# Sixteen experts on 64 slots and two column strips, sixteen on 32 slots and four, with the overflow branch moved behind the sixth quad

## Chip, cores and metric

One NeuronCore of a Trainium2 chip runs the whole program. The metric is device microseconds of one execution, as the median of the runs shown.

## The reference, cut to what matters

Two layers of mixers and a dense feed-forward run first, and then two more layers, each of which ends in a mixture of 32 experts. Only that expert stage is touched. For 256 tokens of width 1024 a router picks one of four groups and in it the two best of eight experts:

```python
def expert_block(args):
    xblk, e = args
    hid = jax.nn.silu(xblk @ w_gate[e]) * (xblk @ w_up[e])
    return hid @ w_down[e]

contrib = weights[order][:, None] * yb[dest]
y = jnp.zeros((t, d)).at[sorted_tok].add(contrib)
```

Gate and up are 1024x512, down is 512x1024, all in float32: 6 MB for one expert, 192 MB for a layer. The 512 assignments of a layer (256 tokens by 2) fall on the 32 experts as the data has it.

## The kernel before

**Slots.** The kernel gives each expert 32 slots (CAP, line 61). Four experts (a quad) share the 128 columns of TensorE: the gathered tokens of expert j are the stationary operand of column strip j (32 columns), and its weights stream through as the moving operand, 512 columns at a time. Each such product is two instructions in the trace. Line 1587 holds gate (`g`) and up (`u`), line 1615 down (`yp`).

**A quad** (`moe`, from line 1520) runs so: `prep` builds a 0/1 matrix `sel` of tokens by slots on VectorE (line 1528) and gathers the tokens with it on TensorE (line 1542, tile `xt` in PSUM, two buffers of tag x); VectorE and ScalarE move the result into `XT` in turn, with the layer's scale and shift (lines 1546, 1548). There is one XT, so the next quad's can be filled only when the last `u` product has read it. `up` makes gate and up, with `combine` of the quad before between them (tile `cb`, line 1635, eight products, added into x by VectorE). `turn` transposes sel (tile `cT`). `hidden` transposes the hidden layer (tile `hTp`, line 1601, also in a buffer of tag x), `down` multiplies it, and `halves` scales the result and splits it in two.

**The weights' stream.** A ring of 1 MB tiles (class Ring, line 181) is filled by SyncE in the order that `plan_second` (line 1115) lists: for each quad gate, up and down, each in two halves of four tiles, one by expert: 24 tiles a quad, 192 a layer. A tile's transfer (line 214) is issued when the tile that many places back has been released, which `done` does behind each half: four tiles at a time. In the expert stage the ring's pools are RING, RING1, RING2 and RING3 (3, 6, 4 and 4 tiles). The first quad has extra work of the layer norm behind its `up` (`late`, line 1876: four products `rowb`, ScalarE copies, GpSimd scaling).

**The branch.** An expert with more than 32 tokens spills. `weights` in `route` (line 1498) leaves the two largest counts and their experts in `mi`. Behind the third quad (XAT = 3, line 49) every engine reads them, and if the largest is over 32, `overflow` (line 1678) loads the weights of those two experts a second time (24 transfers of 0.5 MB, tile `fw`, line 1711) and treats up to 64 further tokens of each on two column strips, through the same `up`, `down` and `combine`. `rest` (line 1723) is for what then still remains. The first gather behind the branch can't be done ahead. In the order of SyncE's queue the branch stands between two of the ring's transfers.

Of the kernel before, what the change touches and what calls it, by code (L numbers as in the profile page):

```python
# [11 lines left out]
F32 = mybir.dt.float32  # L12
F32R = mybir.dt.float32r
# [3 lines left out]
ALU = mybir.AluOpType  # L17
# [3 lines left out]
P = 128  # L21
S = 256
D = 1024
KT = D // P
NT = S // P
# [14 lines left out]
NP = 2  # L40
RING1 = 6
RING2 = 4
RING3 = 4
DP = ((0, 100), (2000, 0))
WB = (0, 0, 3)
PB = (2, 3, 3)
EV = 'avaa'
RINGX = (0, 1)
HIPB = 4
XAT = 3  # L50
HQ = 2
HT = 0
LAG = 2
# [4 lines left out]
HF = 4  # L58
NE = 32
DE = 512  # L60
CAP = 32
QE = 4
XCAP = 64
KEY = 64
ALPHA = (2.0 * DEPTH) ** 0.25
# [10 lines left out]
class Packer:  # L76
# [3 lines left out]
    def add(self, name, width):  # L80
        self.at[name] = (self.n, width)
        self.n += width


def const_layout():
# [162 lines left out]
def v3(a, b):  # L248
    return lambda t: t[:, : a * b].rearrange("p (a b) -> p a b", a=a)


class Kern:
# [60 lines left out]
    p = c  # L313
# [801 lines left out]
    def plan_second(self, i):  # L1115
        ap, ring = self.ap, self.ring
        if i == 0:
            ring.rows(ap["norm_final"])
            w = ap["a_w_in_2"][0].rearrange("(k p) c -> p k c", p=P)
            for g in range(4):  # L1120
                for h in range(2):
                    ring.add((w[:, :, h * D + g * 256 : h * D + (g + 1) * 256], v3(8, 256)))
            wo = ap["a_w_out_2"][0]
        else:
            w = ap["b_w_in_2"][0].rearrange("(k p) c -> p k c", p=P)
            for g in range(4):
                for h in (1, 2, 0):
                    ring.add((w[:, :, h * D + g * 256 : h * D + (g + 1) * 256], v3(8, 256)))
            wo = ap["b_w_out_2"][0]
        wo = wo.rearrange("(k p) c -> p k c", p=P)  # L1130
        for kk in range(4):
            ring.add((wo[:, 2 * kk : 2 * kk + 2, :], v3(2, D)))
        ring.blank()
        for qd in range(NE // QE):
            if qd == NE // QE - 1:
                ring.blank()
            es = range(QE * qd, QE * qd + QE)
            for nm in ("e_w_gate_2", "e_w_up_2"):
                for hf in range(2):
                    for e in es:  # L1140
                        ring.add((ap[nm][i, e].rearrange("(p k) f -> p k f", p=P)[:, 4 * hf : 4 * hf + 4, :], v3(4, DE)))
            for hf in range(2):
                for e in es:
                    ring.add((ap["e_w_down_2"][i, e].rearrange("(p f) d -> p f d", p=P)[:, 2 * hf : 2 * hf + 2, :], v3(2, D)))

    def affine(self, pool, g, b, sc, sh):
        nc = self.nc
# [291 lines left out]
    def route(self, i, pool, pC, rw, csum, crow, stats, meanwhile):  # L1439
        nc = self.nc  # L1440
# [10 lines left out]
        key = pool.tile([P, NE], F32, name="key")  # L1451
# [66 lines left out]
        return R, W, (key, k8, mi), weights  # L1518

    def moe(self, i, pool, A, B, R, W, g1, xs, weights, late, pG, pU, pY, pX, pC):  # L1520
        nc = self.nc
# [10 lines left out]
            return last  # L1532

        def gather(sel):
            XT = v3(KT, P)(pool.tile([P, KT * P], F32, name="XT", tag="XT"))
            for q in range(KT // 4):
                b = pX.tile([P, 4, P], F32, name="xt", tag="x")
                for k in range(4):
                    c0 = (4 * q + k) * P
# [3 lines left out]
                for k in range(4):  # L1543
                    kk = 4 * q + k
# [6 lines left out]
        def slots():  # L1551
            return pool.tile([P, NT, P], F32R, name="sel", tag="sel", bufs=2)

        def prep(qd, then=None):
            sel = slots()
            last = pick(sel, QE, CAP, R, slice(QE * qd, QE * qd + QE))
# [91 lines left out]
            if end and i < DEPTH - 1:  # L1648
                self.scale_x(rows)

        def take(tag, at):
            return (2 if tag == "d" else 4), [self.ring.take() for _ in range(QE)]

        cur = prep(0, weights)
        pend = None
        for qd in range(NE // QE):
# [10 lines left out]
            if qd == 0:  # L1667
                with self.after(last):
                    late()
                src = self.row_src(self.ap["ffn_ln_g_2"][i], self.ap["ffn_ln_b_2"][i])  # L1670
            C, ws = turn(sel, QE, CAP, lambda t, j: W[:, t, QE * qd + j : QE * qd + j + 1])
            if qd + 1 < NE // QE and qd + 1 != XAT:
                cur = prep(qd + 1)
            pend = (C, halves(down(hidden(sl), QE, CAP, take, self.ring.done), ws))
        combine(*pend, end=True)
        self.ring.drop(held)

    def overflow(self, i, pool, A, B, R, W, g1, xs, pG, pU, pY, pX, pC, fns):
        nc, tc = self.nc, self.tc
        pick, gather, slots, turn, up, hidden, down, halves, combine = fns  # L1680
        key, k8, mi = xs
        over = (CAP + 1) * KEY
        rv = nc.values_load(mi[0:1, 2:3], min_val=0, max_val=(S + 1) * KEY)
        with tc.If(rv > over):
            es = [nc.values_load(mi[0:1, j : j + 1], min_val=0, max_val=NE - 1) for j in range(2)]
            oh = pool.tile([P, 2, NE], F32, name="oh", tag="oh")
# [2 lines left out]
            for j in range(2):  # L1689
                nc.vector.tensor_scalar(oh[:, j, :], key, k8[:, j : j + 1], None, op0=ALU.is_equal)  # L1690
                for t in range(NT):
                    nc.vector.scalar_tensor_tensor(junk, R[:, t, :], 1.0, oh[:, j, :], ALU.mult, ALU.mult, accum_out=Rx[:, t, j : j + 1])
                    nc.vector.scalar_tensor_tensor(junk, W[:, t, :], 1.0, oh[:, j, :], ALU.mult, ALU.mult, accum_out=Wy[:, t, j : j + 1])
            nc.vector.tensor_scalar(Rx, Rx, float(-CAP), None, op0=ALU.add)
            sel = slots()
# [23 lines left out]
            gv = nc.values_load(mi[0:1, 3:4], min_val=0, max_val=(S + 1) * KEY)  # L1719
            with tc.If(gv > over):  # L1720
                self.rest(i, pool, A, B, R, W, g1, key, oh, pG, pU, pY, pX)

    def rest(self, i, pool, A, B, R, W, g1, key, oh, pG, pU, pY, pX):
        nc, tc = self.nc, self.tc
        if True:
            scr = pool.tile([P, 7 * NE], F32, name="scr", tag="yl")
# [6 lines left out]
            nc.vector.tensor_scalar(thr, thr, float(XCAP), float(CAP + 1), op0=ALU.mult, op1=ALU.add)  # L1733
# [14 lines left out]
            for t in range(NT):  # L1748
# [3 lines left out]
                    nc.tensor.transpose(b, self.n[:, t, k::KT], self.ident)  # L1752
                    nc.vector.tensor_scalar(h[:, k, :], b, A[:, k : k + 1], B[:, k : k + 1], op0=ALU.mult, op1=ALU.add)
                with tc.For_i(0, NE, 1) as iv:
                    ce = nc.values_load(mi[0:1, 0:1], min_val=-KEY * XCAP, max_val=(S + 1) * KEY)
                    with tc.If(ce > (CAP + 1) * KEY):
# [246 lines left out]
```

## Time and profile before

| | us |
|---|---|
| median of 3 runs (2137.33 to 2144.72) | 2140.43 |
| the profiled execution, its own time | 2138.41 |
| its span in the profile | 2136.6 |
| TensorE busy, share of the span | 1817.5, 85% |
| VectorE busy | 943.2, 44% |
| ScalarE busy | 578.9, 27% |
| read from memory over the span | 607.24 MB, 285 GB/s |

Engines in the rows: PE is TensorE, DVE is VectorE, ACT is ScalarE, POOL is GpSimd, SPq is the queue of SyncE. A row's L number is a line of the kernel. "PEclk" is TensorE's granted clock as a share of 2.4 GHz. The span is the profiler's window of the execution; its times are counted from the span's start.

### The profile page before, as it was taken

How to read it: one execution, taken by the hardware profiler on the slowest of the kernel's cores; microseconds unless marked ns; L12 is line 12 of the kernel's file. 1: busy time of each engine (PE TensorE's matmuls, PEld its weight loads, DVE VectorE, ACT ScalarE, POOL GpSimd, SP SyncE). 2: the span in 40 equal slices, each digit the busy share in tenths (PEclk: the TensorE clock that was granted, in tenths of full speed). 3: DMA queues.
4: the chain of work that ended last, by engine and by line, in shares of the span. 5: the costliest groups of instructions: out<-in, count | busy, mean ns of one | idle time of the engine just before them, and what ended most of it. 6: DMA issues, size and time to landing. Idle time of an engine off the chain costs nothing. (4 is left out here: it accounts for less than half of the span.)

```text
span 2136.6 us, 27574 instructions
## 1 busy us (share of the span) xinstructions
PE 1817.5 (85%) x10962; PEld 1210.9 (57%) x10962; DVE 943.2 (44%) x1935; ACT 578.9 (27%) x1120; POOL 179.0 (8%) x219
## 2 busy tenths in 40 slices
PE   7999999999989997898875588777799977777875
PEld 7887999998879996765312133222398421422221
DVE  6565779564677786874111011111486310111112
ACT  5443544263454332333100010001234200100010
POOL 2210000020100004400100000000240100000000
PEclk9787999996889997997987799999799799799888
DMA  7222979351368993565999659999947699999996
GB/s 221 76 99 80 339 276 375 107 153 37 108 225 284 327 340 122 160 222 215 422 422 423 220 199 423 423 423 422 364 171 302 265 423 422 390 423 422 423 422 271
DMA packets 181708, 611.09 MB, mean 286 GB/s; under 512 B 19392, under 2 KB 105792, under 8 KB 132416
## 3 DMA queue, kind: packets, MB, share of 16 engines
q1 hardware_dynamic: 178368, 605.05, 73.8%
q10 hardware_dynamic: 1872, 2.26, 0.3%
q0 software_dynamic: 1328, 1.90, 0.3%
q8 instruction: 89, 1.46, 0.3%
q14 instruction: 51, 0.42, 0.1%
HBM read 607.24 MB, written 1.93 MB: 285 GB/s over the span
## 5 line engine op out<-in xcount | busy, mean ns | idle before, releaser
L372 DVE TENSOR_TENSOR wlo<-w,whi 128x1024 fp32r<-128x1024 f32 (+3 forms) x232 | 277.5, 1208 | 101.0 <-ACT whi L371 100.1
L371 ACT CAST whi<-w 128x1024 fp32r<-128x1024 f32 (+3 forms) x232 | 224.3, 983 | 230.3 <-PE gu L406 59.4
L1587 PE MATMUL u<-w,XT 128*32 128x512 f32 x1024 | 201.1, 697 | 75.8 <-DMA w<-in_e_w_up_dram 75.7
L1595 DVE TENSOR_TENSOR sl<-sl,u 128x512 f32<-128x512 f32 x17 | 11.7, 687 | 504.7 <-PE u L1587 504.7
L1587 PE MATMUL g<-w,XT 128*32 128x512 f32 x1024 | 191.0, 658 | 33.6 <-DMA w<-in_e_w_gate_dram 33.6
L1615 PE MATMUL yp<-w,sl 128*32 128x512 f32 x1024 | 198.1, 657 | 18.3 <-DMA w<-in_e_w_down_dram 12.8
L1587 PEld LDWEIGHTS u<-w,XT 128*32 128x32 f32 x1024 | 44.5, 125 | 220.4 <-DMA w<-in_e_w_up_dram 139.6
L407 PE MATMUL gu<-hTf,wlo 128*128 128x256 f32 x512 | 146.5, 286 | 0.7 <-DVE wlo L372 0.6
L405 PE MATMUL gu<-hTf,whi 128*128 128x256 f32 x512 | 146.2, 286 | 0.8 <-ACT whi L371 0.8
L406 PE MATMUL gu<-hTf,whi 128*128 128x256 f32 x512 | 145.8, 285 | 0.0
L1625 DVE SCALAR_TENSOR_TENSOR y<-yp,ws,g 128x512 f32<-128x512 f32 x34 | 25.5, 749 | 252.8 <-PE yp L1615 235.4
L1615 PEld LDWEIGHTS yp<-w,sl 128*32 128x32 f32 x1024 | 48.8, 117 | 139.1 <-issue 88.8
L1587 PEld LDWEIGHTS g<-w,XT 128*32 128x32 f32 x1024 | 44.0, 118 | 135.3 <-issue 67.4
L807 DVE SCALAR_TENSOR_TENSOR aacc<-w,ca,aacc 128x1024 f32<-128x1024 f32 x84 | 107.5, 1280 | 2.2 <-DMA w<-in_ada_w_dram 1.5
L405 PEld LDWEIGHTS gu<-hTf,whi 128*128 128x128 f32 x512 | 98.3, 192 | 2.7 <-ACT whi L371 1.2
L406 PEld LDWEIGHTS gu<-hTf,whi 128*128 128x128 f32 x512 | 98.9, 193 | 1.4
L407 PEld LDWEIGHTS gu<-hTf,wlo 128*128 128x128 f32 x512 | 98.1, 192 | 2.4 <-DVE wlo L372 1.1
L1542 PE MATMUL xt<-sel,nhh 128*128 128x128 f32 x272 | 86.1, 340 | 13.3 <-DVE sel L1528 13.3
L1548 ACT ACTIVATE XT<-xt,B,A 128x128 f32<-128x128 f32 x68 | 28.9, 455 | 242.0 <-DVE XT L1546 240.7
L405 PE MATMUL mm<-whi,hT 128*128 128x384 f32 (+2 forms) x256 | 88.8, 354 | 4.6 <-ACT hT L489 4.6
L1542 PEld LDWEIGHTS xt<-sel,nhh 128*128 128x128 f32 x272 | 67.8, 249 | 38.5 <-issue 32.5
L406 PE MATMUL mm<-wlo,hT 128*128 128x384 f32 (+2 forms) x256 | 89.3, 352 | 0.0
(488 smaller groups left out, 3687.7 us busy)
## 6 DMA issues: line engine op xcount, KB each, us to landing
w<-in_e_w_gate_dram SPq DMA_DIRECT2D x128, 1024.0 KB, 19.7
w<-in_e_w_up_dram SPq DMA_DIRECT2D x128, 1024.0 KB, 19.7
w<-in_e_w_down_dram SPq DMA_DIRECT2D x128, 1024.0 KB, 19.7
w<-in_ada_w_dram SPq DMA_DIRECT2D x48, 1024.0 KB, 7.3
w<-in_w_gate_dram SPq DMA_DIRECT2D x22, 1024.0 KB, 6.0
w<-in_w_up_dram SPq DMA_DIRECT2D x22, 1024.0 KB, 7.1
w<-in_w_down_dram SPq DMA_DIRECT2D x22, 1024.0 KB, 6.4
w<-in_w_in_dram SPq DMA_DIRECT2D x16, 768.0 KB, 4.3
```

The source lines that it names most:

```text
L371: self.half_act = nc.scalar.copy(hi, src)
L372: self.half_last = nc.vector.tensor_tensor(lo, src, hi.bitcast(F32), ALU.subtract)
L405: nc.tensor.matmul(out, lhsT=a[0], rhs=b[0], start=start, stop=False)
L406: nc.tensor.matmul(out, lhsT=a[0], rhs=b[1], start=False, stop=False)
L407: self.mm_last = nc.tensor.matmul(out, lhsT=a[1], rhs=b[0], start=False, stop=stop)
L807: nc.vector.scalar_tensor_tensor(acc, w[:, j, :], c, acc, ALU.mult, ALU.add)
L1542: nc.tensor.matmul(b[:, k, :], lhsT=nh[hl][:, t, c0 : c0 + P], rhs=sel[:, t, :], start=t + hl == 0, stop=t + hl == NT)
L1548: nc.scalar.activation(XT[:, kk, :], b[:, k, :], AF.Identity, scale=A[:, kk : kk + 1], bias=B[:, kk : kk + 1])
L1587: last = nc.tensor.matmul(ps[c, :], lhsT=XT[:, kk, c], rhs=wt[j][:, k, :], start=kk == 0, stop=kk == KT - 1, tile_position=(0, w * j))
L1595: nc.vector.tensor_tensor(sl, sl, res[1], ALU.mult)
L1615: nc.tensor.matmul(ps[h][c, :], lhsT=hid[:, ff + f, c], rhs=wt[j][:, f, h * 512 : (h + 1) * 512], start=ff + f == 0, stop=ff + f == 3, til ...
L1625: nc.vector.scalar_tensor_tensor(y[:, c], ps[h], ws, g1[:, c], ALU.mult, ALU.mult)
```

## The change

The first four quads (NWIDE) give each expert 64 slots: such a quad is gathered at once, 256 slots wide, and computed in two steps of two experts, each on two column strips of 64. The other four quads stay as they were. The ring's list follows the steps, and tiles are taken and released two at a time in a wide step. The gather makes four PSUM tiles instead of two for a wide quad. The branch is asked before the quad with number 6 (counted from 0), so behind the sixth and ahead of the last two; it is taken where a count is over 64 in the first sixteen experts or over 32 in the others (`cm` holds the difference). RING3 goes from 4 to 3 tiles. What `overflow` and `rest` compare is adapted to the two capacities.

```diff
-RING3 = 4
+RING3 = 3
-XAT = 3
+XAT = 6
-CAP = 32
+NWIDE = 4
...
+def steps(qd):
+    e = QE * qd
+    return [(e, 2, 64), (e + 2, 2, 64)] if qd < NWIDE else [(e, 4, 32)]
...
+            for e0, n, w in steps(qd):
+                es = range(e0, e0 + n)
+                for nm in ("e_w_gate_2", "e_w_up_2"):
...
-            nc.vector.scalar_tensor_tensor(key, rk[:, 2, :], float(KEY), self.c("rev32"), ALU.mult, ALU.add)
+            nc.vector.memset(cm[:, : QE * NWIDE], 0.0)
+            nc.vector.memset(cm[:, QE * NWIDE :], float(32 - XCAP))
+            nc.vector.tensor_tensor(key, rk[:, 2, :], cm, ALU.subtract)
+            nc.vector.scalar_tensor_tensor(key, key, float(KEY), self.c("rev32"), ALU.mult, ALU.add)
...
-            XT = v3(KT, P)(pool.tile([P, KT * P], F32, name="XT", tag="XT"))
-            for q in range(KT // 4):
-                b = pX.tile([P, 4, P], F32, name="xt", tag="x")
+            z = sel.shape[2]
+            XT = v3(KT, z)(pool.tile([P, KT * z], F32, name="XT", tag="XT"))
+            g = 512 // z
+            for q in range(KT // g):
+                b = pX.tile([P, g, z], F32, name="xt", tag="x")
...
-            sl, last = up(XT, QE, CAP, take, self.ring.done, (lambda: combine(*pend)) if pend else (lambda: None))
+            todo = steps(qd)
+            for m, (e0, n, w) in enumerate(todo):
+                take = lambda tag, at: (2 if tag == "d" else 4, [self.ring.take() for _ in range(n)])
+                c = slice(m * P, m * P + P)
+                sl, last = up(XT[:, :, c], n, w, take, self.ring.done, (lambda: combine(*pend)) if pend else (lambda: None))
...
+                C, ws = turn(sel[:, :, c], n, w, lambda t, j: W[:, t, e0 + j : e0 + j + 1])
+                if m == len(todo) - 1 and qd + 1 < NE // QE and qd + 1 != XAT:
+                    cur = prep(qd + 1)
+                pend = (C, halves(down(hidden(sl), n, w, take, self.ring.done), ws))
...
-        over = (CAP + 1) * KEY
+        over = (XCAP + 1) * KEY
```

## Rows read from the trace of the kernel before

**Rows 1.** The page: bandwidth in 40 equal slices of the span.

```profile
GB/s 221 76 99 80 339 276 375 107 153 37 108 225 284 327 340 122 160 222 215 422 422 423 220 199 423 423 423 422 364 171 302 265 423 422 390 423 422 423 422 271
```

**Rows 2.** Busy time by engine in stretches; last columns: granted clock, DMA share, GB/s.

```profile
690.00:740.00 50.00, 50.00 (x349) 45.84 (x348) 40.70 (x44) 20.88 (x30) 0.98 (x2) 1.00 0.93 323
...
1050.00:1100.00 50.00, 35.42 (x190) 10.19 (x186) 7.46 (x13) 3.87 (x9) 0.00 (x0) 0.95 1.01 423
...
1100.00:1150.00 50.00, 36.22 (x166) 9.02 (x158) 7.82 (x26) 2.42 (x4) 0.00 (x0) 0.88 1.01 422
...
1200.00:1250.00 50.00, 33.26 (x88) 10.19 (x88) 6.95 (x13) 2.42 (x4) 0.00 (x0) 0.92 0.51 164
```

**Rows 3.** The chain that ended last, in order of time: start, length, what.

```profile
2096.71 19.73 DMA w<-in_e_w_down_dram
```

**Rows 4.** SyncE's queue in order of time: start, length, what, count.

```profile
998.41 0.33 SPq L214 DMA_DIRECT2D w<-in_e_w_gate_dram  x1
...
1121.60 17.59 SPq L214 DMA_DIRECT2D w<-in_e_w_gate_dram  x8
...
1324.69 18.10 SPq L214 DMA_DIRECT2D w<-in_e_w_gate_dram  x8
...
1384.53 17.62 SPq L214 DMA_DIRECT2D w<-in_e_w_gate_dram  x8
...
1797.38 17.60 SPq L214 DMA_DIRECT2D w<-in_e_w_gate_dram  x8
...
1920.59 17.80 SPq L214 DMA_DIRECT2D w<-in_e_w_gate_dram  x8
...
1980.16 17.76 SPq L214 DMA_DIRECT2D w<-in_e_w_gate_dram  x8
```

**Rows 5.** Waits of SyncE's queue from 1000 us on: us, times, longest.

```profile
SPq L1684 <- SPq L1684: 19.6, 7, 5.1
```

**Rows 6.** Transfers issued from 865 to 975 us: count, size, median us to landing.

```profile
w<-in_e_w_gate_dram SPq DMA_DIRECT2D x8, 1024.0 KB, 7.3
w<-in_e_w_up_dram SPq DMA_DIRECT2D x8, 1024.0 KB, 8.2
...
w<-in_e_w_down_dram SPq DMA_DIRECT2D x1, 1024.0 KB, 5.3
```

**Rows 7.** TensorE in order of time: start, length, tile, count, idle before.

```profile
700.52 0.28 PE L405 MATMUL gu<-hTf,whi 128*128 128x256 f32 x1
700.63 0.28 PE L406 MATMUL gu<-hTf,whi 128*128 128x256 f32 x1
...
1001.27 6.60 PE L1587 MATMUL u<-w,XT 128*32 128x512 f32 x57
...
1020.28 7.07 PE L1615 MATMUL yp<-w,sl 128*32 128x512 f32 x64
...
1126.57 1.94 PE L1615 MATMUL yp<-w,sl 128*32 128x512 f32 x12 [0.68 <-ACT sl L1603]
...
1222.09 0.65 PE L1587 MATMUL u<-fw,XT 128*64 128x512 f32 x2 [2.23 <-DMA fw<-in_e_w_up_dram]
...
1300.71 0.39 PE L1635 MATMUL cb<-yh,C 128*128 128x512 f32 x1
1300.94 0.40 PE L1635 MATMUL cb<-yl,C 128*128 128x512 f32 x1
...
1302.92 1.04 PE L1587 MATMUL g<-w,XT 128*32 128x512 f32 x2
1303.89 0.44 PE L1565 MATMUL cT<-ident,sel 128*128 128x128 f32 x2
...
1328.44 0.75 PE L1601 MATMUL hTp<-ident,sl 128*128 128x128 f32 x4 [2.66 <-ACT XT L1548]
```

**Rows 8.** Instructions by line from 1050 us on: busy us, mean ns.

```profile
L1635 PE MATMUL cb<-yh,C 128*128 128x512 f32 x64 | 30.1, 483 | 15.9 <-ACT yh L393 9.2 <-DVE x L1641 4.5 <-DVE x L1205 1.1
```

**Rows 9.** As rows 2, for the 3.4 us behind one of TensorE's waits.

```profile
1330.00:1333.40 3.40, 3.40 (x18) 1.57 (x20) 0.00 (x0) 0.00 (x0) 0.00 (x0) 0.58 1.01 419
```

More of the change, by code (lines that the diff above doesn't have):

```diff
@@ L1136, in plan_second @@
                 ring.blank()
-            es = range(QE * qd, QE * qd + QE)
-            for nm in ("e_w_gate_2", "e_w_up_2"):
+            for e0, n, w in steps(qd):
+                es = range(e0, e0 + n)
+                for nm in ("e_w_gate_2", "e_w_up_2"):
+                    for hf in range(2):
+                        for e in es:
+                            ring.add((ap[nm][i, e].rearrange("(p k) f -> p k f", p=P)[:, 4 * hf : 4 * hf + 4, :], v3(4, DE)))
                 for hf in range(2):
                     for e in es:
[L1141 to L1144, printed above, removed]
+                        ring.add((ap["e_w_down_2"][i, e].rearrange("(p f) d -> p f d", p=P)[:, 2 * hf : 2 * hf + 2, :], v3(2, D)))
     def affine(self, pool, g, b, sc, sh):
@@ L1450, in route @@
         R, W = [pool.tile([P, NT, NE], F32, name=n) for n in ("R", "W")]
-        key = pool.tile([P, NE], F32, name="key")
+        key, cm = [pool.tile([P, NE], F32, name=n) for n in ("key", "cm")]
         k8 = pool.tile([P, 8], F32, name="k8")
@@ L1517, in route @@
         gx = tt(1)
-        return R, W, (key, k8, mi), weights
+        return R, W, (key, cm, k8, mi), weights
     def moe(self, i, pool, A, B, R, W, g1, xs, weights, late, pG, pU, pY, pX, pC):
@@ L1534, in gather @@
         def gather(sel):
-            XT = v3(KT, P)(pool.tile([P, KT * P], F32, name="XT", tag="XT"))
-            for q in range(KT // 4):
-                b = pX.tile([P, 4, P], F32, name="xt", tag="x")
-                for k in range(4):
-                    c0 = (4 * q + k) * P
+            z = sel.shape[2]
[3 more added lines that the diff above has]
+                b = pX.tile([P, g, z], F32, name="xt", tag="x")
+                for k in range(g):
+                    c0 = (g * q + k) * P
                     for t in range(NT):
@@ L1542, in gather @@
                             nc.tensor.matmul(b[:, k, :], lhsT=nh[hl][:, t, c0 : c0 + P], rhs=sel[:, t, :], start=t + hl == 0, stop=t + hl == NT)
-                for k in range(4):
-                    kk = 4 * q + k
+                for k in range(g):
+                    kk = g * q + k
                     if k % 2 == 0:
@@ L1549, in gather, with slots @@
             return XT
-        def slots():
-            return pool.tile([P, NT, P], F32R, name="sel", tag="sel", bufs=2)
+        def slots(z):
+            return pool.tile([P, NT, z], F32R, name="sel", tag="sel", bufs=2)
         def prep(qd, then=None):
-            sel = slots()
-            last = pick(sel, QE, CAP, R, slice(QE * qd, QE * qd + QE))
+            w = steps(qd)[0][2]
+            sel = slots(QE * w)
+            last = pick(sel, QE, w, R, slice(QE * qd, QE * qd + QE))
             if then:
@@ L1649, in combine @@
                 self.scale_x(rows)
-        def take(tag, at):
-            return (2 if tag == "d" else 4), [self.ring.take() for _ in range(QE)]
         cur = prep(0, weights)
@@ L1665, in moe @@
             XT, sel = cur
-            sl, last = up(XT, QE, CAP, take, self.ring.done, (lambda: combine(*pend)) if pend else (lambda: None))
[L1667 to L1674, printed above, removed]
+            todo = steps(qd)
[3 more added lines that the diff above has]
+                sl, last = up(XT[:, :, c], n, w, take, self.ring.done, (lambda: combine(*pend)) if pend else (lambda: None))
+                if e0 == 0:
+                    with self.after(last):
+                        late()
+                    src = self.row_src(self.ap["ffn_ln_g_2"][i], self.ap["ffn_ln_b_2"][i])
+                C, ws = turn(sel[:, :, c], n, w, lambda t, j: W[:, t, e0 + j : e0 + j + 1])
+                if m == len(todo) - 1 and qd + 1 < NE // QE and qd + 1 != XAT:
+                    cur = prep(qd + 1)
+                pend = (C, halves(down(hidden(sl), n, w, take, self.ring.done), ws))
         combine(*pend, end=True)
@@ L1680, in overflow @@
         pick, gather, slots, turn, up, hidden, down, halves, combine = fns
-        key, k8, mi = xs
-        over = (CAP + 1) * KEY
-        rv = nc.values_load(mi[0:1, 2:3], min_val=0, max_val=(S + 1) * KEY)
+        key, cm, k8, mi = xs
+        over = (XCAP + 1) * KEY
+        rv = nc.values_load(mi[0:1, 2:3], min_val=0, max_val=(S + XCAP) * KEY)
         with tc.If(rv > over):
@@ L1691, in overflow @@
                 for t in range(NT):
-                    nc.vector.scalar_tensor_tensor(junk, R[:, t, :], 1.0, oh[:, j, :], ALU.mult, ALU.mult, accum_out=Rx[:, t, j : j + 1])
+                    nc.vector.tensor_tensor(junk, R[:, t, :], cm, ALU.subtract)
+                    nc.vector.scalar_tensor_tensor(junk, junk, 1.0, oh[:, j, :], ALU.mult, ALU.mult, accum_out=Rx[:, t, j : j + 1])
                     nc.vector.scalar_tensor_tensor(junk, W[:, t, :], 1.0, oh[:, j, :], ALU.mult, ALU.mult, accum_out=Wy[:, t, j : j + 1])
-            nc.vector.tensor_scalar(Rx, Rx, float(-CAP), None, op0=ALU.add)
-            sel = slots()
+            nc.vector.tensor_scalar(Rx, Rx, float(-XCAP), None, op0=ALU.add)
+            sel = slots(P)
             pick(sel, 2, XCAP, Rx, slice(0, 2))
@@ L1718, in overflow, with rest @@
             combine(C, halves(down(hidden(sl), 2, XCAP, take, nop), ws))
[L1719 removed]
+            gv = nc.values_load(mi[0:1, 3:4], min_val=0, max_val=(S + XCAP) * KEY)
             with tc.If(gv > over):
[L1721 to L1723 removed]
+                self.rest(i, pool, A, B, R, W, g1, key, cm, oh, pG, pU, pY, pX)
+    def rest(self, i, pool, A, B, R, W, g1, key, cm, oh, pG, pU, pY, pX):
         nc, tc = self.nc, self.tc
@@ L1732, in rest @@
             nc.vector.tensor_copy(mi, cf)
-            nc.vector.tensor_scalar(thr, thr, float(XCAP), float(CAP + 1), op0=ALU.mult, op1=ALU.add)
+            nc.vector.tensor_scalar(thr, thr, float(XCAP), float(XCAP + 1), op0=ALU.mult, op1=ALU.add)
+            nc.vector.tensor_tensor(thr, thr, cm, ALU.add)
             for t in range(NT):
@@ L1754, in rest @@
                 with tc.For_i(0, NE, 1) as iv:
-                    ce = nc.values_load(mi[0:1, 0:1], min_val=-KEY * XCAP, max_val=(S + 1) * KEY)
-                    with tc.If(ce > (CAP + 1) * KEY):
+                    ce = nc.values_load(mi[0:1, 0:1], min_val=-KEY * XCAP, max_val=(S + XCAP) * KEY)
+                    with tc.If(ce > (XCAP + 1) * KEY):
                         res = []
```

## The prediction

> **What bounds the kernel now.** I read the page's bandwidth slices first, then busy time by stretch, then the chain that ended last, then SyncE's queue, then TensorE. In both expert stages the bandwidth sits at 422 to 423 GB/s for several slices, with holes at 199 to 220 and at 171 [rows 1]. In such a stretch the DMA share is 1.01 while TensorE is busy for 35 to 36 of 50 us [rows 2]. The chain ends in the weights' transfers: each of its late steps is a ring transfer of nearly 20 us that waits only for another [rows 3]. So the expert stage runs at the speed of the weights' stream. A quad (24 tiles) passes SyncE in 59.84 us in the first such layer (1324.69 to 1384.53) and in 59.57 us in the second (1920.59 to 1980.16) [rows 4], which is 2.49 us a tile.
>
> The hole at 199 GB/s is the overflow branch of the first layer; from 1200 to 1250 us the stream is at 164 GB/s [rows 2]. Its price shows in the queue: from the gate transfers at 1121.60 to those at 1324.69 two quads take 203.09 us [rows 4], which is 203.09 - 2 x 59.84 = **83.4 us** too long. In the second layer the branch isn't taken, and the same stretch (1797.38 to 1920.59) takes 123.21 us, 123.21 - 2 x 59.57 = **4.1 us** too long. That is the price of passing it: SyncE waits out the transfers that are under way (19.6 us in 7 waits [rows 5]) before it issues the next, and the stream runs dry for a moment.
>
> **Part by part.** *The branch.* The trace doesn't tell which experts were overfull. The reference's router on the inputs that it draws does: in the first of the two layers experts 3 and 4 have 34 and 35 tokens and no other over 30, in the second no expert is over 29. Both lie among the sixteen that get 64 slots. So neither layer takes the branch any more: the 24 transfers `fw`, their products and the wait for them go. Passing it costs 4.1 us in each layer, as now in the second. Its place changes little: SyncE again waits for what is under way, and behind it stand the last 32 of 192 transfers (6 quads of 24 and 16 ahead are issued); who waits for those is the seventh quad, whose first 16 tiles have landed or are under way. On VectorE the first `sel`, on TensorE the first gather stand behind the branch, in the new place as in the old. What the fourth quad's gather lost by it, the seventh's loses now. Sum: 83.4 - 4.1 = 79.3 us gained.
>
> *The ring.* Seventeen tiles are issued before the first product of the layer (8 + 8 + 1 [rows 6]), then the stream stands still until the first release at 998.41 [rows 4]. With one tile less, one more has to pass afterwards: 2.5 us a layer. In the steady stretch the ring isn't what limits.
>
> *TensorE in a wide quad.* A phase of a narrow quad (gate, up or down) is 64 instructions on four strips and takes 7.07 us [rows 7], 16 rounds of 0.44. Do two strips run side by side? In the branch, which uses two, two instructions took 0.65 us together, where two on one strip take 1.04 [rows 7]; so yes, and a phase of a wide step is 32 instructions in 16 rounds, again 7.07. A wide quad has six: 42.4. The gather is 32 products of 256 columns; products of that width follow at 0.11 us [rows 7], 3.5. Two combines are 16 products: at their pace of 0.23 us [rows 7] they take 3.7, by busy time (0.47 each [rows 8]) 7.5, since they wait for VectorE in between; neither end is nearer, so I take the middle, 5.6. Two `cT` of 0.44 and two `hTp` of 0.75 [rows 7]: 2.4. Two waits of 0.68 ahead of `yp`: 1.4. Ahead of `hTp` TensorE waits 2.66 us for the evacuation of the next quad's gather [rows 7]; a wide quad has this once, and its four PSUM tiles make it longer by an estimated 0.5; in the other step, without a gather, I put 1.0: together 4.2. Behind such a wait the clock was granted at 0.58 for 3.4 us [rows 9], which costs 1.4. Sum: 42.4 + 3.5 + 5.6 + 2.4 + 1.4 + 4.2 + 1.4 = **60.9 us**, against 59.7 of the stream. What was 23 us of spare time becomes none: the cover of nearly everything in these quads is gone. The overhang is 1.2 x 4 = 4.8 us a layer. From below (combine 3.7, the one wait 2.66, no half clock) a quad takes 56.1 and costs nothing. From above (combine 7.5, 2.66 in both steps, two stretches of half clock) it takes 65.3 and costs 22 us a layer.
>
> The Trainium skill, page "TensorEngine Tiling (Array Packing)", section "Tiling Modes", says that a change of the tiling mode drains TensorE, and a wide quad changes twice as often between strips and the full array. By that rule each of some 8 more changes would leave a product's tail open, 1.04 - 2 x 0.435 = 0.17 us, an estimated 1.4 us a quad and 11 us in all, and the sum would be 2099. Here the transposes `cT` begin at 1303.89, before the strip product ahead of them ends by the records at 1303.96 [rows 7], which shows no drain.
>
> *The first quad.* TensorE frees two tiles at a time now, at half the speed. From the first release to the end of the first step's `up` are three half phases, 10.6 us. From there to the first `yp` it took 12.4 us (1007.87 to 1020.28 [rows 7]), since the layer norm's extra work lies there; then half a phase, 3.5. So 26.5 us pass in which 8 tiles are released, 19.9 us of stream: it runs dry for 6.6 us, or 3.1 if the next quad's gather (32 products of 0.11) no longer lies in that gap, which the two-step quad allows. I take 5, between 2 and 8.
>
> *The start.* `sel` and the first gather are twice as wide, before the first product; no row prices it. It can't gain; by the gather's whole length in its wide form (3.5, of which the narrow one is already paid) it is under 2. I take 1.
>
> The few VectorE instructions of `cm` lie in `weights`, beside the gather: nothing; without that cover they would be well under 1 us.
>
> **The sum.** Costs in a layer: 2.5 + 4.8 + 5 + 1 = 13.3, twice 26.6. Net 79.3 - 26.6 = 52.7 us. The profiled execution took 2138.41, so it would take 2085.7; the median of the runs is 2.0 above it, so **2088 us**. With the lower ends (2.5 + 0 + 2 + 0.5 a layer) it is 2071, with the upper ones (2.5 + 22 + 8 + 2) 2130.
>
> **Rivals.** *TensorE becomes the bound of the wide quads* (0.22): the order of its queue was made for a stage with spare time, and where each step's waits come at their upper values a quad takes 65 us. That is 4 x 4.1 us more in a layer, 33 in all: 2121. For it: only 1.2 us separate the two already. Against it: the sum isn't a low one, with the wait ahead of `hTp` at its measured 2.66 and the combines well above their pace.
>
> *The half clock eats the gain* (0.09, slower). The gain left is 52.7 / 8 = 6.6 us a wide quad. The work at full clock is 53.9 us (all but the waits and the clock's own term); a share s of it done at half clock adds 53.9 s, of which 1.4 is counted, so from s = 0.15, a granted clock of 0.87 over the stage, the change is a loss. At 0.80 (s = 0.25) it costs 12.1 x 8 = 97 us more: 2185. For it: narrow quads show 0.95 and 0.88 [rows 2], and each wait ahead of `hTp` can bring a drop. Against it: where TensorE was busy for 50 of 50 us, the clock was 1.00 [rows 2], and the waits for single transfers, which fill the narrow quads, go.
>
> *The branch is still taken in one layer* (0.04, slower): if the chip's counts differ from the reference's, or stay over 32 in the last sixteen. Then 79.3 come back: 2167. Against it: one layer took it and the other not, as the counts say.
>
> **The numbers.** The forecast, with all from 2066 to 2104, has 0.60; the first rival, up to 2134, 0.22; what lies between it and a loss, 2134 to 2147, 0.05; the two slower rivals 0.13. A measurement of this kernel tells 0.3%, 6.4 us, from no change. So faster 0.82, same 0.05, slower 0.13. The range, 2066 to 2124, takes in most of the first rival and leaves out about 2 in 10, nearly all of it above.
>
> **What would show it.** Right: no `fw` rows in either layer; SyncE's quads at 59 to 61 us in a wide quad, 59.6 in a narrow one, one stretch 4 us longer ahead of the last two; TensorE busy nearly without gaps in the first four quads, at a clock over 0.95; two-strip phases of about 7.1 us; `hTp` waits of 3 us once a quad. Wrong: quads of 64 us and more at SyncE with SPq waiting for TensorE rather than for transfers, a granted clock under 0.87 there, two-strip products following at 0.43 us each instead of in pairs, or a stop in the stream over 8 us at the layer's start.

## The result and the profile after

The changed kernel takes **2091.61 us** (median of 4 runs, 2082.70 to 2095.26); the kernel before took 2142.38 on the same chip (4 runs, 2137.33 to 2144.72). The ratio is 0.976, with a 95% interval of 0.9722 to 0.9797: 51 us faster. 2088 was forecast, with a range of 2066 to 2124. The profiled execution of the changed kernel took 2082.70 us, with a span of 2080.5. It is the fastest of its four, 9 us under their median; the one of before lies 2 us under the median that the prediction used.

The page of the changed kernel: span, and bandwidth in 40 slices (GB/s).

```profile
span 2080.5 us, 27466 instructions
...
GB/s 217 88 102 81 317 259 370 152 156 60 102 169 322 273 351 212 119 169 206 362 423 422 422 322 424 421 390 416 255 196 229 423 422 422 390 339 422 413 400 266
```

The hole at 199 in the first expert stage [rows 1] is gone. In its place stands a shallower one at 322, and the second stage, which had none there, has one too, at 339. The slice at 390 in the first stage is the branch that is asked and passed. In the second stage the 390 belongs to the new hole, and the branch lies in the slices at 413 and 400. So there is a cost of a kind that before didn't have, once in each layer.

The same in stretches: busy time of TensorE, its weight loads, VectorE, ScalarE and GpSimd with their instructions, then granted clock, DMA share, GB/s.

```profile
1000.00:1050.00 50.00, 50.00 (x244) 20.60 (x242) 9.66 (x16) 9.84 (x19) 10.49 (x6) 1.00 1.01 424
1050.00:1100.00 50.00, 47.82 (x228) 21.39 (x226) 14.77 (x24) 7.74 (x16) 0.00 (x0) 0.97 1.01 421
1100.00:1150.00 50.00, 49.04 (x230) 18.54 (x226) 12.21 (x20) 5.12 (x11) 0.00 (x0) 1.00 1.01 422
1150.00:1200.00 50.00, 46.27 (x210) 21.04 (x212) 11.85 (x20) 6.72 (x13) 0.00 (x0) 0.97 1.01 421
1200.00:1250.00 50.00, 47.02 (x238) 18.36 (x240) 9.88 (x18) 4.90 (x12) 0.00 (x0) 0.93 0.82 319
1250.00:1300.00 50.00, 38.60 (x244) 11.83 (x240) 7.45 (x13) 5.06 (x11) 0.00 (x0) 0.90 1.01 424
```

The wide quads are computed from 990 to about 1235 us. TensorE, busy 35 to 36 of 50 us there before [rows 2], is now busy 46 to 50. Yet the stream runs at 421 to 424 GB/s until 1200, from the very first stretch on. Then it loses (421 - 319) / 421 x 50 = **12 us** in one place, where the first narrow quad takes over.

What SyncE's queue waited for from 990 to 1200 us: us in all, times, longest.

```profile
SPq L220 <- PE g L1600: 73.1, 22, 13.1
SPq L220 <- PE yp L1628: 66.0, 15, 10.5
SPq L220 <- PE u L1600: 33.6, 21, 4.1
SPq L220 <- DMA w<-in_e_w_gate_dram: 2.8, 2, 1.7
```

SyncE waits 172.7 us for TensorE's releases and hardly at all for transfers, and still the stream is full: enough transfers were issued ahead. By this row alone one would call TensorE the bound; the GB/s of the same stretch say that it isn't yet. How much is issued ahead shows in the time from a transfer's issue to its landing, first from 1050 to 1100 us, then from 1170 to 1220:

```profile
w<-in_e_w_gate_dram SPq DMA_DIRECT2D x8, 1024.0 KB, 13.4
...
w<-in_e_w_gate_dram SPq DMA_DIRECT2D x8, 1024.0 KB, 7.4
```

At 2.49 us a tile some five transfers are under way in the first stretch and some three in the second, an estimate from these rows. The GB/s up to 1200 are the same, but the cushion of transfers under way shrinks.

SyncE's queue in the changed kernel: start, length, what, count.

```profile
992.93 3.77 SPq L220 DMA_DIRECT2D w<-in_e_w_up_dram  x2
...
1212.45 23.03 SPq L220 DMA_DIRECT2D w<-in_e_w_up_dram  x8
1245.01 6.69 SPq L220 DMA_DIRECT2D w<-in_e_w_down_dram  x8
...
1310.96 17.72 SPq L220 DMA_DIRECT2D w<-in_e_w_gate_dram  x8
...
1374.21 15.17 SPq L220 DMA_DIRECT2D w<-in_e_w_gate_dram  x7
...
1414.54 17.62 SPq L220 DMA_DIRECT2D w<-in_e_w_down_dram  x8
```

From the first release at 992.93 to the end of the last issue, 1414.54 + 17.62, the layer takes **439.2 us**. This length is the measure in all that follows. Before it was 502.9 in the first layer and 423.2 in the second; now it is 439.2 and 441.0. So the expert stages gain 63.7 and lose 17.8, 45.9 us together. The rest of the two spans, 2136.6 - 926.1 = 1210.5 before and 2080.5 - 880.2 = 1200.3 after, differs by 10 us. It is 1205 to 1213 in the nine profiles below that have no more than four wide quads, so one execution differs from another by nearly as much; that this one lies 9 us under its median fits.

### The profile page after: what moved, and what is told of

The parts are those of the page before. It is cut to its first block, busy times and chain, and to the rows that moved or that the text cites. A ratio compares the mean times of both kernels' runs of the same rounds, so it can differ in the third digit from the quotient of the medians.

```text
span 2080.5 us, 27466 instructions
## 1 busy us (share of the span) xinstructions
PE 1869.5 (90%) x10924; PEld 1252.4 (60%) x10924; DVE 985.7 (47%) x1979; ACT 600.5 (29%) x1158; POOL 183.7 (9%) x219
## 5 line engine op out<-in xcount | busy, mean ns | idle before, releaser
L377 ACT CAST whi<-w 128x1024 fp32r<-128x1024 f32 (+3 forms) x232 | 224.2, 983 | 229.0 <-PE gu L412 60.9
L1600 PE MATMUL g<-w,XT 128*64 128x512 f32 (+1 forms) x1024 | 240.4, 631 | 17.7 <-DMA w<-in_e_w_gate_dram 17.7
L1628 PE MATMUL yp<-w,sl 128*64 128x512 f32 (+1 forms) x1024 | 237.3, 631 | 17.8 <-DMA w<-in_e_w_down_dram 10.7
L1600 PE MATMUL u<-w,XT 128*64 128x512 f32 (+1 forms) x1024 | 215.3, 615 | 28.5 <-DMA w<-in_e_w_up_dram 28.5
L1638 DVE SCALAR_TENSOR_TENSOR y<-yp,ws,g 128x512 f32<-128x512 f32 x48 | 35.9, 749 | 293.7 <-PE yp L1628 286.9
L1628 PEld LDWEIGHTS yp<-w,sl 128*64 128x64 f32 (+1 forms) x1024 | 69.9, 129 | 157.1 <-issue 113.2
L1600 PEld LDWEIGHTS u<-w,XT 128*64 128x64 f32 (+1 forms) x1024 | 61.8, 126 | 157.9 <-issue 108.7
L1600 PEld LDWEIGHTS g<-w,XT 128*64 128x64 f32 (+1 forms) x1024 | 63.0, 129 | 136.4 <-issue 100.6
L399 ACT CAST yh<-y 128x512 fp32r<-128x512 f32 x48 | 29.7, 618 | 259.0 <-DVE y L1638 259.0
L1554 PE MATMUL xt<-sel,nhh 128*128 128x256 f32 (+1 forms) x256 | 77.1, 328 | 22.5 <-DVE sel L1538 15.4
L1654 DVE TENSOR_TENSOR x<-x,cb 128x512 f32<-128x512 f32 x88 | 58.1, 685 | 79.5 <-PE cb L1648 79.3
```

The source lines that it names most:

```text
L377: self.half_act = nc.scalar.copy(hi, src)
L399: a = nc.scalar.copy(hi, src)
L1600: last = nc.tensor.matmul(ps[c, :], lhsT=XT[:, kk, c], rhs=wt[j][:, k, :], start=kk == 0, stop=kk == KT - 1, tile_position=(0, w * j))
L1628: nc.tensor.matmul(ps[h][c, :], lhsT=hid[:, ff + f, c], rhs=wt[j][:, f, h * 512 : (h + 1) * 512], start=ff + f == 0, stop=ff + f == 3, til ...
L1638: nc.vector.scalar_tensor_tensor(y[:, c], ps[h], ws, g1[:, c], ALU.mult, ALU.mult)
L1654: nc.vector.tensor_tensor(a, a, b, ALU.add)
```

## The experiments

Layer lengths are given as first/second layer.

### 1. What the branch is worth, what the ring tile, what the place

In the kernel before, the branch asks for a count that no expert reaches, so that it is passed in both layers. The tokens over 32 of the two overfull experts are left out.

```diff
-        over = (CAP + 1) * KEY
+        over = (XCAP + 1) * KEY
```

> The kernel before, with the branch asked behind the third quad as ever, but taken only above 64 tokens, so in neither layer; the tokens over 32 of two experts are left out. My theory, that the whole gain of the change is the branch not taken and that two strips and the shorter ring only cost: 2142 - 79 = 2063 us, the first layer's stretch at the branch 4 us longer than two quads, as in the second. A rival, that the branch was worth less and the other parts of the change gain too: 2085 or more.

Measured: 2058.36 us (2054.26 to 2059.77) against 2139.85 of before, ratio 0.9613 (0.9588 to 0.9639). The layers take 423.1/423.4 us. So the branch taken is worth **81 us** by the medians and 79.8 by the first layer's length (79.3 forecast), and 423 is what a layer takes when the stream alone sets its pace and the branch is passed. The queue of this kernel around the branch, in SyncE's rows:

```profile
1122.07 17.59 SPq L214 DMA_DIRECT2D w<-in_e_w_gate_dram  x8
...
1186.09 3.99 SPq L214 DMA_DIRECT2D w<-in_e_w_gate_dram  x3
```

From gate to gate it is 64.0 us, 4.2 over the 59.84 of a quad: the price of passing the branch, now seen in the first layer.

The ring's tile alone, in the kernel before:

```diff
-RING3 = 4
+RING3 = 3
```

> The kernel before with RING3 at 3, nothing else. My theory: one tile less ahead of each layer, 2.5 us a layer, 2147 us. The rival that the price the change pays (some 16 us a layer) comes from the shorter ring: 2160 to 2170. The other rival, that the tile is hidden: 2142.

Measured: 2144.97 (2134.97 to 2146.94), ratio 1.0017 (1.0002 to 1.0031), layers 505.3/425.9: 2.4 and 2.7 us more, as forecast.

The branch's place alone, in the kernel before, where the first layer still takes it:

```diff
-XAT = 3
+XAT = 6
```

> The kernel before with XAT at 6: the branch behind the sixth quad, still taken in the first layer. My theory: the place is worth nothing, 2142 us within 8. The rival that the later place is part of the gain (fewer transfers of the ring wait behind it): 2100 to 2125.

Measured: 2145.93 (2134.55 to 2149.69), ratio 1.0017 (0.9998 to 1.0036). The layers take 507.8/423.9: the move costs 0.7 us where the branch is passed and 5 where it is taken. The 5 come from one execution, and where the branch is taken such a length scatters by half as much: it is 505.4 in the kernel with nothing but another order (end of section 3). The runs' times don't tell the move from nothing.

### 2. Where the changed kernel's 16 to 18 us go

Against 423.1/423.4 the changed kernel's layers cost 16.1 and 17.6 us more. 2.5 of that is the ring's tile. Is the rest paid in each wide quad, as forecast, or at the change from wide to narrow? First, half as many wide quads (in both layers the overfull experts still lie in them):

```diff
-NWIDE = 4
+NWIDE = 2
```

> The changed kernel with two wide quads instead of four (experts 0 to 7, which hold the two overfull ones). My theory, that TensorE falls behind the stream a little more with each wide quad and that the stop of some 12 us at the first narrow quad is that lag: with two the lag stays inside the ring, the stop goes, 2070 to 2080 us. The rival that the step from two-tile to four-tile releases makes the stop whatever went before: 2091.

Measured: 2066.70 (2060.72 to 2068.64), ratio 0.9648 (0.962 to 0.9675). The layers take 428.9/428.1. Two wide quads less gain 10.3 and 12.9 us, and from 1050 to 1350 us no stretch of 50 us is under 417 GB/s, though the change from wide to narrow is still there. So the change is not costly by itself; it is costly after four wide quads in a row.

Then all four wide quads, but in turn with the narrow ones:

```diff
+ORDER = (0, 4, 1, 5, 2, 6, 3, 7)
...
-def steps(qd):
-    e = QE * qd
-    return [(e, 2, 64), (e + 2, 2, 64)] if qd < NWIDE else [(e, 4, 32)]
+def steps(at):
+    e = QE * ORDER[at]
+    return [(e, 2, 64), (e + 2, 2, 64)] if ORDER[at] < NWIDE else [(e, 4, 32)]
...
-            last = pick(sel, QE, w, R, slice(QE * qd, QE * qd + QE))
+            last = pick(sel, QE, w, R, slice(QE * ORDER[qd], QE * ORDER[qd] + QE))
```

> The changed kernel with the quads in the order 0, 4, 1, 5, 2, 6, 3, 7, so that each wide quad is followed by a narrow one; the same sixteen experts have 64 slots. My theory: a narrow quad leaves TensorE some 25 us of spare time, in which the lag of the wide one before is made up; the stop of 12 us in each layer goes: 2066 to 2078 us. The rival that each change from wide to narrow costs a stop: four of them in a layer, 2110 or more. The rival that the price lies in the ring and the layer's start: 2091.

Measured: 2064.70 (2049.56 to 2070.69) against 2142.29 of before, ratio 0.9626 (0.9579 to 0.9673), layers 427.4/428.9. The same work on the same strips, and 12 us a layer less: what is lost is a **lag that adds up**. TensorE falls behind a little in each wide quad and releases tiles later, more of them wait landed in the ring and fewer are under way (the landing times of the section above), and as long as some are under way the stream doesn't feel it. A narrow quad in between lets TensorE catch up.

The branch not asked at all, so that the treatment of experts with more tokens than slots is left out (there are none here):

```diff
-                self.overflow(i, pool, A, B, R, W, g1, xs, pG, pU, pY, pX, pC, (pick, gather, slots, turn, up, hidden, down, halves, combine))
```

> The changed kernel without the branch's question; what overfull experts would need is left out (there are none over the new limits in these inputs). My theory: passing the branch costs 3.5 to 4 us in each layer, since SyncE waits out the transfers under way and the stream runs dry: 2084 us. The rival that it is hidden behind the stream: 2091.

Measured: 2080.60 (2079.62 to 2082.39), ratio 0.9715 (0.9699 to 0.9731), layers 434.4/436.5: passing costs 4.8 and 4.5 us of the stretch, at its place behind the sixth quad.

### 3. The order inside a wide step

Where the lag shows, TensorE stands as follows in the changed kernel (start, length, tile, count, idle before):

```profile
1120.80 0.75 PE L1614 MATMUL hTp<-ident,sl 128*128 128x128 f32 x4 [0.18 <-DVE sl L1608]
...
1151.55 0.38 PE L1554 MATMUL xt<-sel,nhh 128*128 128x256 f32 x1 [1.99 <-ACT XT L1560]
...
1154.43 1.05 PE L1614 MATMUL hTp<-ident,sl 128*128 128x128 f32 x4
...
1183.57 0.75 PE L1614 MATMUL hTp<-ident,sl 128*128 128x128 f32 x4 [0.85 <-DVE sl L1608]
...
1209.65 7.04 PE L1600 MATMUL u<-w,XT 128*64 128x512 f32 x30
1219.35 0.75 PE L1614 MATMUL hTp<-ident,sl 128*128 128x128 f32 x4 [2.66 <-ACT XT L1560]
...
1222.68 6.04 PE L1628 MATMUL yp<-w,sl 128*64 128x512 f32 x16
```

`u` ends at 1209.65 + 7.04 = 1216.69, and the first half of `yp` that would free tiles ends at 1228.72: 12 us without a release. In it lie the wait of 2.66 us for the evacuation of the next gather, 16 products of a further gather (`xt`), and half a `yp` phase that takes 6.04 us where others take 3.65. That is what the clock does behind the wait, as it did in the kernel before [rows 9]; the same view as rows 9 for the changed kernel:

```profile
1221.00:1228.00 7.00, 7.00 (x23) 3.19 (x24) 0.00 (x0) 0.00 (x0) 0.00 (x0) 0.53 0.70 291
```

A granted clock of 0.53 is, but for the edges, the lower of the two levels (1.2 GHz). The wait is there because `hTp` shares its PSUM tag with the gather and stands behind it in the program. So `hidden` is put ahead of `prep`:

```diff
+                hid = hidden(sl)
                 if m == len(todo) - 1 and qd + 1 < NE // QE and qd + 1 != XAT:
                     cur = prep(qd + 1)
-                pend = (C, halves(down(hidden(sl), n, w, take, self.ring.done), ws))
+                pend = (C, halves(down(hid, n, w, take, self.ring.done), ws))
```

> The changed kernel with the hidden layer's transposes issued ahead of the next quad's gather, so that they no longer wait for a PSUM buffer that the gather holds. My theory, that the 12 us without a release of tiles at a wide quad's end, with the 2.7 us wait ahead of the transposes and the half clock behind it, make the stop at the first narrow quad: TensorE saves some 3 us a wide quad, 2075 to 2086 us. The rival that the scheduler orders TensorE's queue by itself, whatever the order in the program: 2091.

Measured: **2062.53 us** (2060.48 to 2063.87), ratio 0.9628 (0.9611 to 0.9644), layers 427.4/428.0. It was better than expected: it takes away the whole stop. Of this kernel, one `hTp` and the stretch that held the stop:

```profile
1185.47 0.75 PE L1614 MATMUL hTp<-ident,sl 128*128 128x128 f32 x4 [0.85 <-DVE sl L1608]
...
1214.24 0.75 PE L1614 MATMUL hTp<-ident,sl 128*128 128x128 f32 x4 [0.88 <-DVE sl L1608]
...
1218.45 7.14 PE L1628 MATMUL yp<-w,sl 128*64 128x512 f32 x32
```

```profile
1200.00:1250.00 50.00, 47.84 (x325) 21.56 (x321) 9.68 (x18) 6.76 (x15) 0.00 (x0) 1.00 1.01 423
```

The wait is 0.88 instead of 2.66, the clock stays at 1.00, and the stream at 423 GB/s. From 1170 to 1220 us, where the changed kernel's gate transfers took 7.4 us to land, they take 12.0, so the cushion is still there:

```profile
w<-in_e_w_gate_dram SPq DMA_DIRECT2D x8, 1024.0 KB, 12.0
```

This version beats both kernels, with the whole computation in it, as the order in turn does too (2064.70, no different by the noise): 29 us under the changed kernel's median, 4 us above the kernel that never takes the branch.

Both together, in turn and with `hidden` ahead (the two edits as above):

```diff
+ORDER = (0, 4, 1, 5, 2, 6, 3, 7)
...
+                hid = hidden(sl)
                 if m == len(todo) - 1 and qd + 1 < NE // QE and qd + 1 != XAT:
                     cur = prep(qd + 1)
```

> Both the order of wide and narrow quads in turn and the transposes ahead of the gather. My theory, that each of the two alone already takes away the same stop at the first narrow quad: nothing more to gain, 2060 to 2066 us, as with one of them. The rival that they save different things: 2040 to 2050.

Measured: 2066.22 (2063.66 to 2069.57) against 2140.89, ratio 0.9667 (0.9639 to 0.9694), layers 427.8/427.6. The edits don't add: each removes the same stop, and there is nothing behind it to gain. And `hidden` ahead of `prep` in the kernel before:

```diff
+            hid = hidden(sl)
             if qd + 1 < NE // QE and qd + 1 != XAT:
                 cur = prep(qd + 1)
-            pend = (C, halves(down(hidden(sl), QE, CAP, take, self.ring.done), ws))
+            pend = (C, halves(down(hid, QE, CAP, take, self.ring.done), ws))
```

> The kernel before with the transposes ahead of the gather, nothing else. My theory: narrow quads leave TensorE over 20 us of spare time, so nothing comes of it: 2142 us within 5. The rival that the order gains by itself, in any quad: 2125 or less.

Measured: 2138.04 (2132.17 to 2140.73), ratio 0.9994 (0.9979 to 1.0008): nothing, as expected of an engine with 14 us of 50 to spare. So the order pays only where TensorE is the slower one.

### 4. Wide quads to the end: two misses

If a wide quad costs so little, all eight could be wide:

```diff
-NWIDE = 4
+NWIDE = 8
...
-            nc.vector.memset(cm[:, QE * NWIDE :], float(32 - XCAP))
```

> The changed kernel with all eight quads wide. My theory, that a wide quad takes TensorE 61 to 62 us against 59.7 of the stream: the stop at the first narrow quad goes, but four more quads run at TensorE's speed, about 2 us each in a layer: 2091 + 16 - 10, so 2090 to 2110 us, and SyncE waits for TensorE in all quads. The rival that TensorE at two strips keeps up and that only the step to narrow quads costs: 2065 to 2075.

Measured: 2153.11 (2150.83 to 2154.87) against 2142.29, ratio 1.0053 (1.0036 to 1.007): half a per cent slower than before, a miss. The layers take 461.0/461.7 us. From the end of the fourth wide quad on the stream is under 422 GB/s:

```profile
1200.00:1250.00 50.00, 46.99 (x212) 19.21 (x212) 14.01 (x23) 7.16 (x15) 0.00 (x0) 0.97 0.99 405
```

The next two stretches of 50 us run at 397 and 413, and the one with the branch at 324. So the cushion is used up after four quads and TensorE sets the pace. The same with `hidden` ahead of `prep`:

```diff
-NWIDE = 4
+NWIDE = 8
...
+                hid = hidden(sl)
                 if m == len(todo) - 1 and qd + 1 < NE // QE and qd + 1 != XAT:
                     cur = prep(qd + 1)
```

> All eight quads wide, with the transposes ahead of the gather. My theory: with all wide and the gather first TensorE took 62 to 63 us a quad against 59.7 of the stream, and the ring's cushion of 16 tiles was used up after four; with the transposes first a quad takes 57 to 59, so the stream bounds again: 2066 to 2090 us, 60 to 85 below the run with all quads wide. The rival that two strips are too slow for eight quads however they are ordered: 2130 or more.

Measured: 2134.54 (2128.76 to 2138.53) against 2140.89, ratio 0.9973 (0.9954 to 0.9992). That was the second miss: 44 us and more above what was expected. The layers take 456.8/449.4. The view shows what a wide quad costs once the layer's start is past; `hTp` of one step in three quads in a row, where SyncE waits for TensorE:

```profile
1188.85 0.75 PE L1613 MATMUL hTp<-ident,sl 128*128 128x128 f32 x4 [0.85 <-DVE sl L1607]
...
1250.03 0.75 PE L1613 MATMUL hTp<-ident,sl 128*128 128x128 f32 x4 [0.85 <-DVE sl L1607]
...
1311.20 0.76 PE L1613 MATMUL hTp<-ident,sl 128*128 128x128 f32 x4 [0.85 <-DVE sl L1607]
```

They are 61.2 us apart, still 1.5 above the stream. And the branch, in the stretch from 1350 us on, for this kernel:

```profile
1300.00:1350.00 50.00, 45.01 (x202) 16.61 (x200) 8.84 (x13) 5.71 (x12) 0.00 (x0) 1.00 1.01 420
1350.00:1400.00 50.00, 40.96 (x186) 19.29 (x187) 13.09 (x22) 5.44 (x12) 0.00 (x0) 0.93 0.80 322
```

(420 - 322) / 420 x 50 = 11.7 us are lost, where passing it cost about 4. In every kernel a gather has to be made behind the branch before any tile is released; here the engine that makes it is already late. To see whether that is the branch, this kernel without it, so that tokens over 64 are left out (there are none). The edit also lets the gather be made ahead, so it doesn't part the branch from the gather behind it:

```diff
-XAT = 6
+XAT = 8
```

> All quads wide, transposes ahead of the gather, and no branch asked (XAT beyond the last quad, so every gather is done ahead); what overfull experts would need is left out. In the run with the branch the stream stood still for some 11 us there in each layer, against 4 with four wide quads. My theory, that this is TensorE's lag laid bare where SyncE waits out its transfers: without the branch 11 us a layer come back, 2134 - 22 = 2112 us, within 8, and the rest of the 70 us above four wide quads is lag that stays. The rival that the branch costs 4 us whatever lag there is, and the lag shows elsewhere instead: 2126.

Measured: 2113.49 (2110.34 to 2116.46) against 2140.86, ratio 0.9877 (0.9859 to 0.9896): 21 us less than with the branch, the expected total. The layers take 445.1/444.9. The first is 11.8 us shorter than with the branch, and its stretch that lost 11.7 us reads:

```profile
1350.00:1400.00 50.00, 46.66 (x211) 18.20 (x212) 9.12 (x14) 5.51 (x12) 0.00 (x0) 1.00 0.98 401
```

The second layer doesn't bear the theory out. Its stream had lost as much at the branch, but its length falls by 4.5 us only (449.4 to 444.9), which is what the rival gave: without the branch the lag shows elsewhere, and the same stretch is slow still. First with the branch, then without:

```profile
1990.00:2040.00 50.00, 43.13 (x204) 19.56 (x206) 9.80 (x17) 6.04 (x13) 0.00 (x0) 0.93 0.81 327
...
1990.00:2040.00 50.00, 48.35 (x207) 18.70 (x203) 11.03 (x17) 8.53 (x16) 0.00 (x0) 1.00 0.89 354
```

The rest of the difference lies outside both lengths: 1227 us there in both kernels with the branch and 1219 in this one, about as much as one execution differs from another (1205 to 1213 above). So 11 us a layer are shown in one layer of two, and the total that came out doesn't prove them. What is left, 445 against 423 us in the layer, was not traced: the ring's tile (2.5) and eight quads at 61.2 instead of 59.7 (12) make 14.5 of the 22.

## Why the prediction was right, and where it was not

**The branch** was read rightly: neither layer takes it, and 81 us were measured where 79.3 had been worked out from two distances in SyncE's queue. Passing it was put at 4.1; the changed kernel shows 1374.21 - 1310.96 = 63.25 us, 3.5 over a quad, and not asking it gains 4.8 and 4.5 in the layer. Its **place** was costed at nothing and costs 0.7 us where it is passed. The claim that behind it nothing is late holds only while TensorE has time to spare (section 4).

**The ring's tile** was right to 0.2 us.

**Two strips side by side** was right: a phase that isn't interrupted takes 7.04 us in the changed kernel, as one on four strips did.

**TensorE in a wide quad** was put at 60.9 us. In the first layer of the changed kernel it is 1183.57 - 1120.80 = **62.8** (section 3). In the second layer it is more:

```profile
1666.24 0.64 PE L1614 MATMUL hTp<-ident,sl 128*128 128x128 f32 x4
...
1730.10 0.75 PE L1614 MATMUL hTp<-ident,sl 128*128 128x128 f32 x4 [0.85 <-DVE sl L1608]
...
1795.51 0.75 PE L1614 MATMUL hTp<-ident,sl 128*128 128x128 f32 x4 [0.85 <-DVE sl L1608]
```

These are quads of 63.9 and **65.4** us. With `hidden` ahead it is 61.2 (section 4), though my terms give 60.9 - 1.4 - 2.5 = 57.0 for that version, without half clock and with 1.7 instead of 4.2 ahead of `hTp`. So the size of the sum was right to 3% in the first layer and to 7% in the second, and its parts were too low by some 4 us where the queue is in order. What the order costs, 62.8 - 61.2 = 1.6 us in that quad, was rightly put down to the wait for the gather's evacuation (1.99 us in that quad, 2.66 in the next) and the clock behind it, and counted as work that can't be avoided; that two lines take it away I didn't ask.

**The step that failed** is "the overhang is 1.2 x 4 = 4.8 us a layer", together with "the first quad: I take 5". A quad's overhang was charged as if the stream felt it at once. In the first layer it doesn't: the first quad shows no stop at all (424 GB/s from 1000 to 1050), and the stretches up to 1200 run at 421 to 422, because released tiles are under way ahead of need and the lag only makes them fewer. All of the lag comes due in one place, as 12 us, when the last wide step has no release for 12 us. In the second layer, with its longer quads, the loss is spread over the last wide quad (the slices at 390 and 339). 4.8 + 5 were charged, 12 paid: the sum of the layer was 13.3 and is 16.1 and 17.6. In the first quad the 12.4 us up to the first `yp`, taken over from the narrow quad, are not empty; the second step's gate products run there:

```profile
1003.32 5.36 PE L1600 MATMUL g<-w,XT 128*64 128x512 f32 x22
```

The total hardly shows the error, since two charges that were not paid stand against one that was missing: in that part the hit is luck. With the measured costs of the layers and the branch's 81 in place of the forecast ones the sum is 2088 + 2.8 + 4.3 - 1.7 = 2093.

**The start** was put at 1 us; of the first layer's extra, 16.1 - 2.5 (the tile) - 12.1 (the stop) = 1.5 us is left, which leaves room for it; it wasn't measured by itself.

**The rivals.** TensorE as the bound at 65 us a quad: the quads came near it, with 62.8 us in the first layer (1219.35 - 1154.43 = 64.9 from the second step of the third quad to that of the fourth) and 63.9 and 65.4 in the second, but its price of 33 us wasn't paid, since the transfers under way covered most of the lag of four quads; with eight wide quads TensorE became the bound indeed. The half clock: no, the granted clock is 0.93 to 1.00 in the wide stage, where 0.87 was the point of loss; but where it did fall, it fell in the place that the stop is made of. The branch still taken: no; no `fw` row is left.

**The drain.** By the rule of the Trainium skill's page "TensorEngine Tiling (Array Packing)", section "Tiling Modes", that a change of the tiling mode drains TensorE, 2099 would have come out. Rows of the changed kernel, two-strip products, then the combine on the full array, then strips again:

```profile
1109.69 1.02 PE L1600 MATMUL g<-w,XT 128*64 128x512 f32 x2
1110.64 0.51 PE L1648 MATMUL cb<-yl,C 128*128 128x512 f32 x1
...
1111.22 0.39 PE L1648 MATMUL cb<-yl,C 128*128 128x512 f32 x1
1111.54 3.65 PE L1600 MATMUL u<-w,XT 128*64 128x512 f32 x16
```

By the ends of these records nothing stands between the changes: `cb` starts at 1110.64 while `g` ends at 1110.71, and `u` starts at 1111.54 while `cb` ends at 1111.61. But the ends are modelled, and the prediction read the same from an end, so only the starts count. By them the two products `g`, a round of 0.44 us, hold the array 1110.64 - 1109.69 = 0.95 us. The all-wide kernel with `hidden` ahead shows it for a gate phase that `cb` and `cT` cut, beside half a phase without a cut:

```profile
1198.50 1.07 PE L1599 MATMUL g<-w,XT 128*64 128x512 f32 x2
1199.50 0.50 PE L1647 MATMUL cb<-yl,C 128*128 128x512 f32 x1
...
1202.05 3.65 PE L1599 MATMUL g<-w,XT 128*64 128x512 f32 x14
1205.63 0.44 PE L1577 MATMUL cT<-ident,sel 128*128 128x128 f32 x2
...
1206.25 3.64 PE L1599 MATMUL g<-w,XT 128*64 128x512 f32 x16
1209.71 7.04 PE L1599 MATMUL u<-w,XT 128*64 128x512 f32 x32
```

Eight rounds without a change take 1209.71 - 1206.25 = 3.46 us, 0.43 each. One round ahead of `cb` takes 1.00 and seven ahead of `cT` take 3.58, each over half a microsecond more than its rounds. Added up so from start to start, without the waits, the strip products of the quad from 1188.85 to 1250.03 take 45.4 us, where six phases were put at 42.4. So a phase that full-array work cuts costs time here, and that far the trace agrees with the rule; these 3.0 us are most of the 4.2 by which the terms fall short of 61.2. The prediction put the rule at 1.4 us a quad and set it aside. Whether it is a drain, or strip products that no longer run in pairs where a phase is cut, the records don't tell.

**Not settled:** the remaining 1.2 us of a wide quad; and the 4 us by which the three best versions stay above a layer of 423, of which 2.5 are the ring's tile. A fourth tile of RING3 together with the wide gather wasn't tried.

## What to carry to other kernels

An engine that is a few per cent slower than the stream it follows costs nothing for as long as enough released tiles are under way, and then most of it in one place, where its releases pause: charge the lag to that place, and ask how many quads the ring can carry, not what one costs. Such a lag is removed as well by mixing slow and fast steps as by making the slow ones faster, and doing both gains nothing more. When an engine loses its spare time, waits that cost nothing before (here `hTp` behind a gather that shares its PSUM buffers, and a branch ahead of which no gather can be made) are the first to look at. And time a phase from start to start where other work cuts it: a phase on strips that is cut costs more than its products.

## What the hardware showed that was not expected

The clock's level after a pause matters most where it delays a release: behind a wait of 2.66 us the granted clock was 0.53 for 7 us, and half a `yp` phase took 6.04 us instead of 3.65; behind waits of 0.85 to 0.88 us, two in each wide quad of the version with `hidden` ahead, it stayed at 1.00 from 1000 to 1250 us. And a branch that isn't taken has no fixed price: passing it cost 3.5 to 4.8 us of stream with up to four wide quads, and with eight, where TensorE was the late one, taking it and the gather behind it away made the layer 11.8 us shorter in the first layer and 4.5 in the second.
